# Branch A of a hybrid attention trunk: one softmax over the keys of three groups, with layouts swapped by small matmuls on TensorE

## The chip, the cores and the metric
One core of one Trainium2 chip runs the whole program. The metric is the device time of one execution in microseconds (us), as a median over runs. PE is the engine of matmuls (TensorE), DVE is VectorE, ACT is ScalarE, POOL is GpSimd, and SP issues the DMAs.

## What is computed
Two layers over 512 tokens of width 1024, batch 1, all in fp32. Each layer normalizes and modulates x, projects it once (w_in), and runs two branches on the result. Branch A, which the change touches, is attention with 8 heads of 64 in each of three groups with different windows and dilations; the groups' results are mixed per query by their softmax denominators. From the reference:

```python
A_PATTERNS = ((128, 1), (512, 4), (2048, 16))
...
    s = jnp.where(valid[None, None, :, None], s + bias, NEG_INF)
    m = jnp.max(s, axis=-1, keepdims=True)
    p = jnp.exp(s - m)
    l = jnp.sum(p, axis=-1, keepdims=True)
    o = jnp.einsum('bpnhqk,bpnkhd->bpnqhd', (p / l).astype(v.dtype), vw)
    lse = (m + jnp.log(l))[..., 0]
...
    wts = jax.nn.softmax(jnp.stack(lses), axis=0)
    o = jnp.sum(jnp.stack(outs).astype(jnp.float32) * wts[..., None], axis=0)
```

Weighting the groups by a softmax of lse = m + log l is the same as one softmax over all keys of the three groups: the sum of exp(s - M) v over all groups, divided by the sum of exp(s - M). Branch B is latent attention with 16 heads. Gates, the two output projections, a merge and w_o follow, and x is added.

## The kernel before
Activations lie transposed, with channels on partitions and tokens along the free axis. Matmul operands are split into a high and a low part in fp32r, so that a product takes three matmuls (hi x hi, hi x lo, lo x hi), and nearly every PSUM result is evacuated twice: ACT (or DVE) copies the high part, DVE subtracts it for the low part. PSUM has tags with few banks: pj 2 (projections), s 3 (scores), t 2 (transposes, statistics), o 1 (results).

A layer runs branch A in four passes, j = 0 to 3, each with two heads (e = 0, 1) of all three groups. a_qk(j) projects queries and keys, six projections of 24 matmuls each, from bank pj; line 663 writes the low part of a key of groups 1 and 2, line 671 of a query of those groups. a_v projects values, zgate the gate z. a_attn(j) then calls a_scores, a_factors and, for each head, a_pv and o_evac, and multiplies by z.

Group 0 is in the order of tokens: queries are split into four blocks of 128 consecutive tokens. Groups 1 and 2 are in the order of phases: block p holds the tokens 4i + p. Within a block of group 0 the queries are ordered so that partition 32p + a holds phase p. So a statistic of query block qb, phase p lies on partitions 32p.. in column qb for group 0, and on partitions 32qb.. in column p for groups 1 and 2. swap_blocks (line 812) goes from one layout to the other by sixteen copies of 32 partitions, twelve on DVE and four on POOL.

In a_scores each group takes its own maximum (line 779 adds the bias and takes the maximum of group 0 in one DVE instruction, line 797 that of groups 1 and 2), and ACT computes the exponentials with that maximum and sums them along the way (lines 783 and 803). a_factors joins the two maxima and sums of groups 1 and 2 (lines 822 to 827), swaps them, joins them with group 0 (lines 831 to 846), swaps the common factor back and forms three factors per query. a_pv scales every block of the probabilities with its factor (scaled, line 859; on DVE, POOL and ACT by the table SE), transposes the blocks on PE (line 866), splits them into pth (line 211) and ptl (line 869), and multiplies with the values in bank o.

The instructions of each engine stand in the order that a scheduler gives them when the program is built, by its own estimate of durations; so work of the next a_qk stands between the steps of a_attn. An engine takes them strictly in that order. Line 166 is the helper of every matmul, line 211 and 213 the copies of high parts, lines 203, 205 and 206 split loaded weights (206 is the subtraction, mostly on POOL).

## Time and profile before

| what | us |
| --- | --- |
| median of 3 runs (1478.69 to 1481.86) | 1481.09 |
| the profiled execution, its own time | 1478.29 |
| its span, first to last instruction | 1476.5 |
| PE busy in it | 1369.5 |
| DVE busy | 1004.1 |
| ACT busy | 624.0 |
| POOL busy | 601.3 |

The span is 1.8 us under the profiled execution's own time, which is 2.8 us under the median. Branch A of layer 0 lies at about 120 to 450 us of the span, that of layer 1 at about 800 to 1150 us. The passes of a_factors are at 173, 228, 366, 417, 883, 941, 1067 and 1117 us. Busy times of engines overlap; a matmul's record is longer than the distance to the next one, since matmuls are pipelined.

### The profile page before, as it was taken

Reading aid. Unit: us, or ns where it says so; the run is one execution under the profiler, and the core shown is the slowest. Engines: PE = TensorE matmul, PEld = TensorE weight load, DVE = VectorE, ACT = ScalarE, POOL = GpSimd, SP = SyncE. Lnnn points to the kernel's source line nnn. Section 1 sums busy time; section 2 is a strip of 40 time slices with the busy share of each in tenths; the row PEclk is TensorE's granted clock in tenths of the full one; section 3 lists DMA queues with packets and bytes.
Section 4 is the critical chain, followed back from the end, with each engine's and each line's share of the span. In section 5 each row is a group of like instructions: output and inputs, shape, how many; then the busy total and the mean of one; then the engine's idle time right before and its main releaser. Section 6 shows DMA issues by size and latency. Waiting matters only on the chain.

```text
span 1476.5 us, 21392 instructions
## 1 busy us (share of the span) xinstructions
PE 1369.5 (93%) x7327; PEld 1161.5 (79%) x7327; DVE 1004.1 (68%) x2477; ACT 624.0 (42%) x1493; POOL 601.3 (41%) x493
## 2 busy tenths in 40 slices
PE   5998898999998998999989999899999899899997
PEld 4786686897777787888888987789777778788877
DVE  8788759345776888764699347734576688885563
ACT  3423552325245767621034254323534566762101
POOL 4423435234463323245544344533446433335530
PEclk7999999999999999999999999999999999999999
DMA  9776414232244333355654322233323442345551
GB/s 323 230 232 189 140 44 117 81 85 79 59 116 122 99 94 95 117 178 171 199 159 135 102 86 71 67 88 86 79 72 110 116 115 79 94 120 188 171 150 58
DMA packets 236677, 181.48 MB, mean 123 GB/s; under 512 B 16410, under 2 KB 204224, under 8 KB 236568
## 3 DMA queue, kind: packets, MB, share of 16 engines
q1 hardware_dynamic: 236568, 180.11, 41.2%
q8 instruction: 58, 0.95, 0.3%
q14 instruction: 51, 0.42, 0.1%
HBM read 150.60 MB, written 23.17 MB: 118 GB/s over the span
## 4 chain that ended last, share of the span: by engine, by line
PE 62%; DVE 21%; ACT 4%; issue 4%; DMA 4%; POOL 3%; SPq 1%; DVEq 0%; POOLq 0%; ACTq 0%
PE pj L166 41%; PE s L166 14%; PE o L166 4%; PE t L866 3%; ACT p L803 2%; DVE mn L812 2%; POOL wl L206 2%; DVE ptl L869 1%; DVE p L1098 1%; DVE lat L286 1%; DVE zs L286 1%; DVE wh L205 1%; DMA stage<-in_w_o 1%; DMA stage<-in_w_in 1%; DVE fp L812 1%
## 5 line engine op out<-in xcount | busy, mean ns | idle before, releaser
L206 POOL TENSOR_TENSOR wl<-stage,wh 128x1024 fp32r<-128x1024 f32 (+1 forms) x134 | 316.7, 2364 | 353.5 <-ACT wh L203 188.8
L166 PE MATMUL pj<-hTh,wh 128*128 128x512 f32 (+1 forms) x864 | 346.5, 401 | 44.7 <-DVE kb L663 19.9
L166 PE MATMUL pj<-hTl,wh 128*128 128x512 f32 (+1 forms) x864 | 339.4, 394 | 0.0
L166 PE MATMUL pj<-hTh,wl 128*128 128x512 f32 (+1 forms) x848 | 336.9, 397 | 0.0
L166 PEld LDWEIGHTS pj<-hTh,wh 128*128 128x128 f32 x864 | 166.2, 192 | 85.1 <-issue 31.8
L166 PEld LDWEIGHTS pj<-hTl,wh 128*128 128x128 f32 x864 | 165.9, 192 | 32.6 <-issue 0.3
L166 PEld LDWEIGHTS pj<-hTh,wl 128*128 128x128 f32 x848 | 163.2, 192 | 29.6 <-issue 0.2
L203 ACT ACTIVATE wh<-stage 128x1024 fp32r<-128x1024 f32 (+1 forms) x84 | 85.1, 1014 | 155.4 <-PE s L166 62.7
L869 DVE TENSOR_TENSOR ptl<-t,pth 128x512 fp32r<-128x512 f32 (+2 forms) x160 | 95.9, 615 | 44.0 <-ACT pth L211 43.4
L211 ACT ACTIVATE pth<-t 128x512 fp32r<-128x512 f32 (+2 forms) x160 | 80.8, 537 | 63.2 <-PE t L866 61.9
L166 PE MATMUL s<-kb,qh 128*128 128x256 f32 (+3 forms) x384 | 86.3, 317 | 7.6 <-DVE mm L1098 3.6
L166 PE MATMUL o<-pth,v 128*64 128x128 f32 (+3 forms) x496 | 88.7, 256 | 3.3 <-DVE kh L920 1.9
L166 PE MATMUL o<-ptl,v 128*64 128x128 f32 (+2 forms) x320 | 77.2, 275 | 6.8 <-DVE ptl L869 6.3
L866 PE MATMUL t<-eye_r,p 128*128 128x128 f32 x560 | 80.1, 275 | 2.7 <-DVE ptl L869 1.0
L166 PEld LDWEIGHTS s<-kb,qh 128*128 128x128 f32 x384 | 65.0, 189 | 18.7 <-DVE mm L1098 6.2
L1098 DVE CUSTOM_DVE_ANT_0 p<-s,cs 128x512 f32<-128x512 f32 (+3 forms) x128 | 58.5, 484 | 25.9 <-PE s L166 25.4
L205 DVE CAST wh<-stage 128x1024 fp32r<-128x1024 f32 (+1 forms) x77 | 57.2, 743 | 25.4 <-PE s L166 8.4
L166 PEld LDWEIGHTS o<-pth,v 128*64 128x64 f32 (+1 forms) x496 | 63.7, 150 | 9.7 <-DVE kh L920 3.2
L866 PEld LDWEIGHTS t<-eye_r,p 128*128 128x128 f32 x560 | 63.2, 140 | 9.9 <-DVE p L859 2.4
L166 PE MATMUL pj<-wh,hTh 128*128 128x256 f32 (+1 forms) x192 | 63.3, 331 | 3.5 <-DVE p L972 1.8
L166 PE MATMUL pj<-wl,hTh 128*128 128x256 f32 (+1 forms) x192 | 62.4, 327 | 1.0 <-DVE wl L206 0.8
L166 PEld LDWEIGHTS o<-ptl,v 128*128 128x128 f32 (+1 forms) x320 | 50.8, 159 | 14.8 <-DVE ptl L869 10.4
(711 smaller groups left out, 3088.1 us busy)
## 6 DMA issues: line engine op xcount, KB each, us to landing
stage<-in_w_in SPq DMA_DIRECT2D x118, 512.0 KB
lat<-in_w_ada SPq DMA_DIRECT2D x64, 256.0 KB
v<-in_w_ada SPq DMA_DIRECT2D x32, 256.0 KB
stage<-in_w_in SPq DMA_DIRECT2D x32, 256.0 KB
gd<-gt SPq DMA_DIRECT2D x32, 256.0 KB
stage<-in_w_out_b SPq DMA_DIRECT2D x16, 512.0 KB
stage<-in_w_o SPq DMA_DIRECT2D x16, 512.0 KB
p<-yd SPq DMA_DIRECT2D x24, 256.0 KB
```

The lines of the kernel that those rows point to most:

```text
L166: T.matmul(o, l, r, start=start, stop=stop, skip_group_check=True)
L203: A.activation(dst_h, src, AF.Copy)
L205: hi.tensor_copy(dst_h, src)
L206: (lo or G).tensor_tensor(dst_l, src, f32(dst_h), ALU.subtract)
L211: A.activation(dst, src, AF.Copy)
L286: V.scalar_tensor_tensor(acc, st, cact[:, k:k + 1], side if k == ne + np_ else acc, ALU.mult, ALU.add)
L803: A.activation(pt[e][:, sl], pt[e][:, sl], AF.Exp, bias=m12[:, g - 1, e, p:p + 1], scale=SA, accum_out=l12[:, g - 1, e, p:p + 1])
L812: (A.copy if c == "A" else (G if c == "G" else V).tensor_copy)(dst[32 * p:32 * p + 32, :, qb], src[32 * qb:32 * qb + 32, :, p])
L866: T.transpose(tp[:, 128 * b:128 * b + 128], s, eye)
L869: V.tensor_tensor(lo[:, :n], tp[:, :n], f32(h[:, :n]), ALU.subtract)
L1098: V.tensor_tensor_reduce(pt, o, mask[:, 512 - n:512], 1.0, -3e38, ALU.add, ALU.max, m[:, qb:qb + 1])
```

## The change
In a_scores, groups 1 and 2 now come first, then group 0. The maximum over groups 1 and 2 (mx) goes into the layout of group 0 by swapped(): DVE multiplies it into ex with a mask (quad) that leaves each value in one of four columns by its quarter of the partitions, and one fp32 matmul with the 0/1 matrix blk (1 where two partitions agree modulo 32) sums over the quarters, so that every quarter holds all values; four instructions of 32 partitions then pick what they need straight from PSUM. M is the maximum over all three groups, its negated and scaled form nM goes back by a second swapped() (nM12), and all exponentials use it: those of group 0 with nM, those of groups 1 and 2 with nM12. No block of probabilities is scaled. a_factors and swap_blocks are gone. a_inverse adds the sums of the groups (with a third swapped()), takes the reciprocal, transposes it (8 x 128), and spreads it with four fp32 matmuls (rowsel is 0/1, 8 rows) over the 128 partitions of the result's layout, in PSUM; the gate z is multiplied by that before it multiplies the result. Three constant tables come with it, in cs (blk, quad) and in rowsel, and the reserve in SBUF for DMA descriptors is set to 1024 bytes a partition.

```diff
+        def swapped(v):
+
+            ex = small([128, 2, 4, 4], "ex")
+            st = list(v.ap[0])
+            a = bass.AP(tensor=v.tensor, offset=v.offset, ap=[st, [4, 2], [1, 4], [0, 4]])
+            m = bass.AP(tensor=quad.tensor, offset=quad.offset, ap=[list(quad.ap[0]), [0, 2], [0, 4], [1, 4]])
+            V.tensor_tensor(ex, a, m, ALU.mult)
+            ps_ = bank("t")
+            mm(ps_[:, :32], blk, ex.rearrange("p e c b -> p (e c b)"), True, True)
+            r = ps_[:, :32].rearrange("p (e c b) -> p e c b", e=2, c=4)
+            return [(slice(32 * c, 32 * c + 32), r[32 * c:32 * c + 32, :, c, :]) for c in range(4)]
...
-                V.tensor_scalar(m0[:, e, :], x0, -SA, None, ALU.mult)
-                for qb, pc, c0, n in G0_BLOCKS:
-                    A.activation(pp[pc][:, c0:c0 + n], pp[pc][:, c0:c0 + n], AF.Exp, bias=m0[:, e, qb:qb + 1],
-                                 scale=SA, accum_out=l0[:, e, qb:qb + 1])
-                pps[e] += pp
...
+            mx = small([128, 2, 4], "mx")
+            V.tensor_tensor(mx, x12[:, 0], x12[:, 1], ALU.max)
+            other = swapped(mx)
...
+            M = small([128, 2, 4], "M")
+            for r, v in other:
+                V.tensor_tensor(M[r], x0[r], v, ALU.max)
+            nM = small([128, 2, 4], "nM")
+            V.tensor_scalar(nM, M, -SA, None, ALU.mult)
+            nM12 = small([128, 2, 4], "nM12")
+            for r, v in swapped(nM):
+                V.tensor_copy(nM12[r], v)
+            l0, l12 = small([128, 2, 4], "l0"), small([128, 2, 2, 4], "l12")
+            for e in range(2):
+                for g in (1, 2):
+                    pt = pps[e][1 + g]
                     for p in range(4):
                         sl = slice(128 * p, 128 * p + 128)
-                        A.activation(pt[e][:, sl], pt[e][:, sl], AF.Exp, bias=m12[:, g - 1, e, p:p + 1],
+                        A.activation(pt[:, sl], pt[:, sl], AF.Exp, bias=nM12[:, e, p:p + 1],
                                      scale=SA, accum_out=l12[:, g - 1, e, p:p + 1])
...
+                for qb, pc, c0, n in G0_BLOCKS:
+                    pt = pps[e][pc][:, c0:c0 + n]
+                    A.activation(pt, pt, AF.Exp, bias=nM[:, e, qb:qb + 1], scale=SA, accum_out=l0[:, e, qb:qb + 1])
+            return pps, l0, l12
+
+        def a_inverse(l0, l12):
+
+            V.tensor_tensor(l12[:, 0], l12[:, 0], l12[:, 1], ALU.add)
+            for r, v in swapped(l12[:, 0]):
+                V.tensor_tensor(l0[r], l0[r], v, ALU.add)
+            V.reciprocal(l0, l0)
+            tp = bank("t")
+            T.transpose(tp[:8, :128], l0.rearrange("p e t -> p (e t)"), eye)
+            rw = small([8, 128], "rw")
+            V.tensor_copy(rw, tp[:8, :128])
+            bc = bank("t")
+            for t in range(4):
+                mm(bc[:, 128 * t:128 * t + 128], rowsel[:, 128 * t:128 * t + 128], rw, t == 0, t == 3)
+            return bc
...
-            for pc in range(2):
-                scaled(pp[pc], [(c0, n, f0[:, qb:qb + 1]) for qb, pc_, c0, n in G0_BLOCKS if pc_ == pc], SE[pc])
...
-                scaled(pp[1 + g], [(128 * p, 128, f12[:, g - 1, p:p + 1]) for p in range(4)], SE[1 + g])
...
-            pps = a_scores(j, qk, stat)
-            f0, f12 = a_factors(stat)
+            pps, l0, l12 = a_scores(j, qk)
+            zn = z.rearrange("d (t a q) -> d t q a", t=4, q=4)
             for e in range(2):
-                o = a_pv(e, pps[e], f0[:, e], f12[:, :, e], vt, 2 * (j % 2) + e)
+                o = a_pv(e, pps[e], vt, 2 * (j % 2) + e)
+                if e == 0:
+                    V.tensor_tensor(zn, zn, a_inverse(l0, l12).rearrange("d (t q a) -> d t q a", t=4, q=4), ALU.mult)
                 o_evac(y, e, o, True)
...
-    nc = bacc.Bacc("TRN2", target_bir_lowering=False, num_devices=1)
+    nc = bacc.Bacc("TRN2", target_bir_lowering=False, num_devices=1, dynamic_dma_scratch_size=1024)
```

The scheduler moves more than the diff shows. In what follows, numbers behind a name tell buffers apart, and line numbers of the changed kernel are its own.

On DVE, in the first pass of layer 0, the twelve copies of the first swap stand ahead of the low part of a key (kb, line 663):

```order
L812 COPY mn_1362<-ml_1353 32x4 x12
L663 TENSOR_TENSOR kb_447<-pj_1740,kb_444 64x4x128
L213 CAST kb_444<-pj_1740 64x4x128
L831 TENSOR_TENSOR M_1379<-m_265_1232,mn_1362 128x8
L663 TENSOR_TENSOR kb_447<-pj_1740,kb_444 64x4x128
L833 TENSOR_TENSOR en_1381<-M_1379,m_265_1232 128x8
L834 TENSOR_TENSOR en_1381<-M_1379,mn_1362 128x8
```

In the changed kernel, at the same key (line 670 there), after the maximum:

```order
L694 TENSOR_TENSOR k_353_1643<-pj_1616,kh_1641 64x512
L820 TENSOR_TENSOR M_1327<-x_280_1294,t_1292 32x8 x4
L822 TENSOR_SCALAR nM_1332<-M_1327 128x8
L768 TENSOR_TENSOR ex_1335<-nM_1332,cs 128x32
L694 TENSOR_TENSOR k_353_1643<-pj_1616,kl_1642 64x512
L825 COPY nM_291_1334<-t_1337 32x8 x4
L670 TENSOR_TENSOR kb_448<-pj_1691,kb_445 64x4x128
L217 CAST kb_445<-pj_1691 64x4x128
L670 TENSOR_TENSOR kb_448<-pj_1691,kb_445 64x4x128
```

Ahead of the key now stand the four maxima of 32 partitions (M), the negation, the product with the mask (ex), the low part of a key of the next pass's group 0, and the four copies from PSUM (nM).

On ACT, at the same place before, the exponentials of groups 1 and 2 (line 803) stand ahead of the high part of that key (kb) and of a query (qh); those of group 0 were done before them:

```order
L803 ACTIVATE p_1286,l_268_1235<-p_1286,m_267_1234 128x128 x4
L803 ACTIVATE p_1287,l_268_1235<-p_1287,m_267_1234 128x128 x4
L277 ACTIVATE lat_1851<-lat_1851,cact 128x512
L203 ACTIVATE wh_1806<-stage_1804 128x1024
L803 ACTIVATE p_1320,l_268_1235<-p_1320,m_267_1234 128x128 x4
L803 ACTIVATE p_1321,l_268_1235<-p_1321,m_267_1234 128x128 x4
L824 ACTIVATE ed_1355<-ed_1355 128x16
L211 ACTIVATE kb_444<-pj_1740 64x4x128
L203 ACTIVATE wh_2242<-stage_2240 128x1024
L211 ACTIVATE qh_1800<-pj_1775 128x512
```

In the changed kernel, from the second head's exponentials of group 0 (line 836) on; those of groups 1 and 2 are line 832:

```order
L836 ACTIVATE p_1313,l_294_1343<-p_1313,nM_1332 128x256 x2
L836 ACTIVATE p_1314,l_294_1343<-p_1314,nM_1332 128x256
L836 ACTIVATE p_1314,l_294_1343<-p_1314,nM_1332 128x128
L215 ACTIVATE kb_445<-pj_1691 64x4x128
L207 ACTIVATE wh_2142<-stage_2140 128x1024
L832 ACTIVATE p_1240,l_295_1344<-p_1240,nM_291_1334 128x128 x4
L832 ACTIVATE p_1264,l_295_1344<-p_1264,nM_291_1334 128x128 x4
L832 ACTIVATE p_1241,l_295_1344<-p_1241,nM_291_1334 128x128 x4
L832 ACTIVATE p_1265,l_295_1344<-p_1265,nM_291_1334 128x128 x4
L215 ACTIVATE pth_1375<-t_1370 128x512
L215 ACTIVATE pth_1387<-t_1383 128x384
L215 ACTIVATE qh_1751<-pj_1726 128x512
```

The key's copy moved in between the two blocks of exponentials, and the query's copy (qh) behind both, and behind two copies of transposed blocks (pth).

On PE, the first transposes of the pass's probabilities stood 73 projection matmuls behind its last score:

```order
L166 MATMUL pj_2246<-hTl_219,wh_2242 128x512
L166 MATMUL pj_2246<-hTh_220,wh_2242 128x512
L866 MATMUL t_1419<-eye_r,p_1245 128x128
L866 MATMUL t_1419<-eye_r,p_1244 128x128 x3
L866 MATMUL t_1432<-eye_r,p_1244 128x128
L866 MATMUL t_1432<-eye_r,p_1245 128x128 x2
L166 MATMUL pj_2246<-hTh_220,wl_2243 128x512
```

In the changed kernel they stand seven matmuls behind the second swapped() (t<-ex), which itself stands 24 projection matmuls behind the pass's last score, one of group 0:

```order
L170 MATMUL t_1337<-ex_1335,cs 128x32
L170 MATMUL pj_1726<-hTh_210,wh_1722 128x512
L170 MATMUL pj_1726<-hTh_210,wl_1723 128x512
L170 MATMUL pj_1726<-hTl_211,wh_1722 128x512
L170 MATMUL pj_1726<-hTh_212,wh_1722 128x512
L170 MATMUL pj_1726<-hTh_212,wl_1723 128x512
L170 MATMUL pj_1726<-hTl_213,wh_1722 128x512
L170 MATMUL pj_1726<-hTh_214,wh_1722 128x512
L868 MATMUL t_1370<-eye_r,p_1298 128x128
L868 MATMUL t_1370<-eye_r,p_1297 128x128 x3
L170 MATMUL pj_1726<-hTh_214,wl_1723 128x512
```

The transposes moved forward, from 73 to 31 projection matmuls behind the last score, and the matmul with ex is new. Matmuls and projections of the latent-attention stages stand as before.

## Rows read from the trace of the kernel before

**Rows 1.** The page's engines (busy us, share, instructions), and its chain by engine.
```profile
PE 1369.5 (93%) x7327; PEld 1161.5 (79%) x7327; DVE 1004.1 (68%) x2477; ACT 624.0 (42%) x1493; POOL 601.3 (41%) x493
...
PE 62%; DVE 21%; ACT 4%; issue 4%; DMA 4%; POOL 3%; SPq 1%; DVEq 0%; POOLq 0%; ACTq 0%
```

**Rows 2.** Windows: us, then each engine's busy us (instructions), PEclk, DMA share, GB/s.
```profile
170.00:300.00 130.00, 116.09 (x623) 95.85 (x622) 84.83 (x228) 48.98 (x125) 51.46 (x56) 0.95 0.32 90
...
450.00:740.00 290.00, 276.73 (x1434) 231.33 (x1434) 210.89 (x469) 138.12 (x315) 115.08 (x85) 1.00 0.46 135
```

**Rows 3.** PE's waits: us in total, times, longest us.
```profile
PE pj L166 <- DVE kb L663: 21.5, 10, 4.5
...
PE o L166 <- DVE ptl L869: 6.3, 13, 1.0
```

**Rows 4.** PE's timeline at eight gaps: start us, us, instruction [idle before <-releaser].
```profile
181.06 0.77 PE L166 MATMUL pj<-hTh,wh 128*128 128x512 f32 x1 [4.46 <-DVE kb L663]
...
237.03 0.57 PE L166 MATMUL pj<-hTh,wh 128*128 128x512 f32 x1 [3.87 <-DVE kb L663]
...
253.49 0.47 PE L166 MATMUL pj<-hTh,wh 128*128 128x512 f32 x1 [1.92 <-DVE kb L663]
...
373.44 0.47 PE L166 MATMUL pj<-hTh,wh 128*128 128x512 f32 x1 [1.89 <-DVE kb L663]
...
889.72 0.47 PE L166 MATMUL pj<-hTh,wh 128*128 128x512 f32 x1 [1.40 <-DVE kb L663]
...
898.29 0.50 PE L166 MATMUL pj<-hTh,wh 128*128 128x512 f32 x1 [1.26 <-DVE ql L671]
...
956.68 0.47 PE L166 MATMUL pj<-hTh,wh 128*128 128x512 f32 x1 [4.08 <-DVE kb L663]
...
1074.11 0.47 PE L166 MATMUL pj<-hTh,wh 128*128 128x512 f32 x1 [1.90 <-DVE kb L663]
```

**Rows 5.** Timeline of DVE and POOL at the first swap of layer 0.
```profile
173.20 4.38 DVE L812 COPY mn<-ml 32x4 f32<-32x4 f32 x12
...
174.45 2.38 POOL L206 TENSOR_TENSOR wl<-stage,wh 128x1024 fp32r<-128x1024 f32 x1 [0.37 <-POOL mn L812]
...
177.61 0.68 DVE L663 TENSOR_TENSOR kb<-pj,kb 64x512 fp32r<-64x512 f32 x1
```

**Rows 6.** Tile mn: engine op xcount: duration ns min/median/max, first and last start us, forms.
```profile
L812 DVE COPY mn<-ml x96: 160/164/2403, 173.2 to 1118.9; 32x4 f32<-32x4 f32 x96
```

**Rows 7.** Windows behind PE's gaps and one at full clock; columns as in rows 2.
```profile
181.06:186.06 5.00, 5.00 (x12) 3.94 (x13) 4.65 (x25) 0.21 (x1) 1.93 (x6) 0.50 0.39 105
...
186.20:191.20 5.00, 5.00 (x23) 4.13 (x22) 3.55 (x13) 2.82 (x6) 4.05 (x7) 1.00 0.00 0
...
237.26:240.67 3.41, 3.41 (x9) 2.64 (x9) 3.38 (x12) 1.10 (x3) 0.40 (x1) 0.50 0.72 193
...
957.47:960.88 3.41, 3.41 (x10) 2.63 (x9) 0.84 (x2) 0.00 (x0) 3.33 (x3) 0.50 0.38 100
```

**Rows 8.** Groups of DVE and ACT by form: xcount | busy us, mean ns.
```profile
L812 DVE COPY mn<-ml 32x4 f32<-32x4 f32 x96 | 27.5, 287 | 1.4
...
L812 DVE COPY fp<-fn 32x2 f32<-32x2 f32 x96 | 19.3, 201 | 1.5
...
L803 ACT ACTIVATE p<-p,m 128x128 f32<-128x128 f32 x128 | 49.6, 389 | 23.3 <-DVE m L799 23.2
...
L783 ACT ACTIVATE p<-p,m 128x256 f32<-128x256 f32 x48 | 23.9, 499 | 22.4 <-DVE m L781 22.1
...
L211 ACT ACTIVATE pth<-t 128x512 fp32r<-128x512 f32 x112 | 63.4, 592 | 62.3 <-PE t L866 61.4
```

**Rows 9.** PE's timeline: fp32 matmuls at full clock, early in the program.
```profile
47.60 0.95 PE L166 MATMUL t<-one_r,zs 128*128 128x1 f32 x8
...
64.98 1.68 PE L166 MATMUL t<-yy,rb 32*24 32x512 f32 x4
```

**Rows 10.** The page's costliest groups: GpSimd's subtraction.
```profile
L206 POOL TENSOR_TENSOR wl<-stage,wh 128x1024 fp32r<-128x1024 f32 (+1 forms) x134 | 316.7, 2364 | 353.5 <-ACT wh L203 188.8
```

96 lines of the change are left out of this document (29 added, 67 removed).

## The prediction

> **What bounds the kernel now.** I first read the engine summary and the chain that ended last: PE is busy for 1369.5 of 1476.5 us and holds 62% of the chain, against 21% for DVE [rows 1]. So time is what PE does plus what PE waits. The busy times by stretch then separate the stages: in the first branch-A stage of layer 0 (170 to 300 us) PE stands idle for 130.00 - 116.09 = 13.9 us, over a tenth, while in the latent-attention stage (450 to 740 us) it stands idle for 13.3 us in 290 [rows 2]. The list of PE's waits says for whom: first comes DVE's line 663, the low part of a projected key, which must be read out of a pj bank before PE may start the next projection; 21.5 us in 10 waits [rows 3]. PE's timeline has eight gaps beside the eight passes through a_factors: 4.46, 3.87, 1.92 and 1.89 us in layer 0, and 1.40, 1.26, 4.08 and 1.90 us in layer 1, 20.8 us together [rows 4]. Seven are line 663, one is line 671, the same work for a query.
>
> Why line 663 is late stands in the timeline of DVE at 173 us [rows 5]. It is queued behind the twelve 32-partition copies of swap_blocks, 4.38 us of DVE, and starts at 177.61, the moment they end. A copy of this tile takes 164 ns at the median but up to 2403 [rows 6], and twelve at the median would be 2.0 us: the other 2.4 us of the 4.38 are those for which GpSimd worked on a 128x1024 subtraction, from 174.45 for 2.38 us [rows 5]. The four larger gaps come with the copies of that first swap, or with the second swap and the row scalings behind it.
>
> A gap costs more than itself. [...] Beside the a_factors passes there are 5.00 us at 0.50 from 181.06, and four stretches of 3.41 us (the first and the last are [rows 7], the others start at 254.33 and 373.80): 18.6 us in which PE did 12/23 of the work, so 18.6 x 0.48 = 8.9 us lost.
>
> **What the change takes away.** Both swaps go, and with them twelve plus twelve DVE copies per attention, 27.5 + 19.3 us over eight attentions [rows 8], some twenty small DVE operations, and every row scaling of the probabilities, which ran on DVE, ACT and POOL. The order of the changed kernel has line 663 behind four short PSUM copies where it had the twelve. I therefore cancel all eight gaps, -20.8 us, and their slow clock, -8.9 us. The rest of DVE's saved time I cost at nothing: PE had no gap there, because projections covered it.
>
> **What it adds on PE.** Nothing that PE did is removed, and PE is the bound, so each added matmul counts in full. Per attention: three products of the 128x128 matrix blk with 32 columns; one transpose; four spreading matmuls with 8 rows and 128 columns. These are fp32, not fp32r. The trace holds two records for an fp32 matmul: four program matmuls with one column are eight records, 0.95 us [rows 9], so 0.24 us each; I take that for a product, 3 x 0.24 = 0.72. The four records of a 32-row fp32 matmul took 1.68 us for 2 x (512 + 384) = 1792 columns [rows 9], 0.94 ns a column; spreading passes 4 x 2 x 128 = 1024 columns, 0.96 us. The transpose is one record, 0.95/8 = 0.12 us. Together 1.8 us, and with eight attentions +14.5 us. From below this is 0, if all of it falls into waits that remain; from above it is twice as much, 29 us, were every added matmul to run at the lower clock; I stay at the row's value because the products stand among projections that keep PE busy. [...]
>
> **What it adds as waits.** The exponentials now share one maximum. All 24 of an attention start only after scores, maximum, product, maximum, and, for groups 1 and 2, a second product. Before, the eight of group 0 could run ahead of the rest. ACT's part is 16 x 0.389 + 6 x 0.499 + 2 x 0.389 = 10.0 us in two blocks, 3.8 and 6.2 [rows 8]. What must not wait behind them is ACT's copy of the next projection (pth and qh in the order of ACT). In the first attention I count from the negated maximum: 3.8 (eight exponentials), 0.6 for kb, 1.1 for one weight cast, 6.2, then two copies of transposed blocks and qh, 0.6 each, and 0.7 on DVE: free after 14.2 us (an ACT copy of a transposed block is 592 ns [rows 8], a weight cast of 1024 columns taken as nearly twice that, DVE's part 0.68 us [rows 5]). PE meanwhile has from the last score 24 projection matmuls, the product, then 48 more, 7 transposes and a few scores before it needs the bank: 72 x 0.217 (5.00/23 [rows 7]) = 15.6, plus some 1.6 for the others at 0.12 each, 17.2 us from the last score. The maximum comes about 2 us after the last score (one reduction, five short operations at about 0.2 us [rows 8], and other work between). Slack: about 1 us. So no systematic wait, but little room. I charge one wait per attention of the kind that the latent-attention stage shows for the same handover, PE for DVE's ptl: 6.3 us in 13 waits, 0.48 us [rows 3]; eight of them, with a little for the bank of tag t that a product holds until the maximum is read, +5 us. Bounds: 0 (cover holds) and 22 us (first rival).
>
> DVE's new operations are 21 short ones and one 512-column product per attention, about 21 x 0.2 + 0.7 = 4.9 us (a short copy of fp took 201 ns on the mean, the 0.7 is line 663's for 512 columns), less than the 5.9 us of the copies alone ((27.5 + 19.3)/8 [rows 8]), and no PE projection waits for the 512-column product. One more DMA, rowsel, and 132 more columns of cs are loaded once, long before use. The smaller reserve for DMA descriptors is at nothing: the loads are issued by SP, and no row shows a use of it. In the latent-attention stages PE's order is that of before, so there I expect no change.
>
> **Sum.** -20.8 - 8.9 + 14.5 + 5 = -10.2. The profiled execution took 1478.29 us (1476.5 us of span and 1.8 around it), 2.8 us under the median of three runs, 1481.09. From the median: **1471 us**.
>
> **Rivals.**
> 1. *ACT's block becomes the wait* (slower). If the maximum arrives late against PE, so that the eight exponentials of group 0 no longer hide, the bank comes 3.8 us later, PE waits 3.8 - 1.0 = 2.8 us in each attention, 22 us in place of the 5: 1488 us. It decides from the point where the maximum is more than that 1 us later than I count. For it: the slack is small, and PE will arrive earlier once its own gaps are gone. Against: in the order of the changed kernel 48 projection matmuls stand between the second product and the first use of the blocks that need it, and ACT is busy for only 624 us [rows 1].
> 2. *The small operations are caught by GpSimd* (no change). A DVE copy stood up to 2.4 us where GpSimd subtracted [rows 5, 6]. The change keeps six such SBUF operations per attention in front of the products (maximum, three products with quad, a sum, a negation), 48 in all. GpSimd's subtraction fills 316.7 of 1476.5 us, 21%, 2364 ns each [rows 10], so an operation meets one with chance 0.21 and stands half of it: 48 x 0.21 x 1.18 = 12 us; if PE waits for all that on top of the forecast: 1483 us. Against it: the median copy of the swap took 164 ns [rows 6], so most were not held, and projections cover the product. [...]
> 3. *The added matmuls fall into remaining waits*, and no new wait comes: -5 - 7 against the sum, 1459 us.
>
> **How the numbers follow.** The forecast (1463 to 1478) has 0.60, rival 3 0.15, rival 1 0.13, rival 2 0.12, of which I put 0.02 with slower. A difference under about 3 us (0.2%) can't be told from none. So faster 0.75, same 0.10, slower 0.15. The range for 8 in 10 goes from a little under rival 3 to a little over rival 1: 1457 to 1490 us.
>
> **What would show it.** Right: line 663 gone from the head of PE's waits, branch-A stretches 29 us shorter in gaps and slow clock but PE's busy time up by 10 to 20 us, DVE's busy time down by tens of us, no granted clock of 0.50 after the first 150 us of layer 0 except at the seams of layers. Wrong by rival 1: PE waiting on ACT's copies or on line 671 behind exponentials, 2 us or more, once per attention. Wrong by rival 2: short operations of over 1 us on DVE ahead of each product, with PE waiting at t<-ex. Wrong on the price: the fp32 records longer than 0.12 us apart.

## The result, and the profile after

The changed kernel takes **1494.47 us** (median of 4 runs, 1489.08 to 1496.09) where the kernel before takes 1481.47 us beside it: ratio 1.0075, 95% interval 1.0048 to 1.0101. It is slower by 13 us; the forecast was 10 us faster. Measured once more beside other kernels the ratio was 1.0076 (1.0062 to 1.0091).

The page's engines and its chain by engine, of the kernel after:

```profile
PE 1389.2 (93%) x7447; PEld 1178.2 (79%) x7447; DVE 956.5 (64%) x2197; ACT 613.0 (41%) x1445; POOL 540.7 (36%) x365
...
PE 70%; DVE 16%; DMA 4%; issue 4%; ACT 3%; SPq 2%; POOL 2%; DVEq 0%; ACTq 0%; POOLq 0%
```

Against [rows 1], DVE is busy for 48 us less and its share of the chain has fallen from 21% to 16%, as the change intended. But PE is busy for 19.7 us more, and its idle time, span less busy time, has fallen only from 107.0 to 1493.6 - 1389.2 = 104.4 us. PE's waits in the kernel after (us in total, times, longest us; helper lines stand four to seven lines further down than before, so that line 663 is now 670, 671 is 678, and 687 is 694):

```profile
PE o L170 <- DVE ptl L871: 8.6, 15, 1.0
...
PE pj L170 <- DVE k L694: 6.7, 2, 4.8
...
PE pj L170 <- DVE ql L678: 5.4, 4, 4.1
PE pj L170 <- DVE ex L768: 4.4, 1, 4.4
...
PE pj L170 <- DVE kb L670: 1.7, 2, 1.3
```

The head of [rows 3], line 663 with 21.5 us, has shrunk to 1.7 us in two waits (line 670). In its place stand other reads of projections (a group-0 key in line 694, a query in line 678) and a product's input (line 768), each with one gap of more than 4 us. The new idle time doesn't come once per attention: branch A has seven gaps of more than 1 us, 20.9 us together, and they belong to five of the eight attentions. These are five of the seven (the others are 1.47 and 1.98 us, at 423 and 1137 us):

```profile
226.67 0.79 PE L170 MATMUL pj<-hTh,wh 128*128 128x512 f32 x1 [4.80 <-DVE k L694]
...
247.81 0.47 PE L170 MATMUL pj<-hTh,wh 128*128 128x512 f32 x1 [4.09 <-DVE ql L678]
...
878.28 0.77 PE L170 MATMUL pj<-hTh,wh 128*128 128x512 f32 x1 [4.38 <-DVE ex L768]
...
940.88 0.42 PE L170 MATMUL o<-lat,one_r 128*2 128x512 f32 x1 [2.24 <-DVE yy L919]
...
943.64 0.80 PE L170 MATMUL pj<-hTh,wh 128*128 128x512 f32 x1 [1.92 <-DVE k L694]
```

The slow clock is there again. Two windows (columns as in [rows 2]), one that begins inside the gap before 878.28 and one that begins between the two gaps around 941, show the granted clock at 0.50 for 6.83 us each; PE worked at that level for 4.80 and 4.91 us of them, against 5.00 and 3.41 us in [rows 7].

```profile
876.25:883.08 6.83, 4.80 (x11) 3.80 (x12) 2.68 (x4) 3.83 (x16) 1.87 (x2) 0.50 0.28 77
941.11:947.94 6.83, 4.91 (x12) 3.44 (x11) 5.19 (x11) 3.25 (x12) 3.94 (x3) 0.50 0.39 98
```

Over the whole span the time at this lower level went from 65.1 to 81.4 us. A second profile of the changed kernel has 75.8 us, with 104.6 us of idle time, so the figure at the lower level varies by some us between executions of one kernel.

How such a gap comes about is read from three engines at 873 us, in the first attention of layer 1. First PE, from the pass's last score (s) on: two projection matmuls, and behind the gap the one at 878.28 that is shown above. Then DVE, then GpSimd:

```profile
872.91 0.32 PE L170 MATMUL s<-k,ql 64*128 64x128 f32 x1
873.16 0.50 PE L170 MATMUL pj<-hTh,wl 128*128 128x512 f32 x1
873.50 0.40 PE L170 MATMUL pj<-hTl,wh 128*128 128x512 f32 x1
```

```profile
873.27 0.29 DVE L815 CUSTOM_DVE_ANT_0 p<-s,bias 128x128 f32<-128x128 f32 x1 [3.06 <-PE s L170]
873.49 0.08 DVE L815 DVE_READ_ACCUMULATOR2_ANT x<- 128x1 f32 x1
873.49 0.68 DVE L694 TENSOR_TENSOR k<-pj,kh 64x512 fp32r<-64x512 f32 x1
874.09 0.67 DVE L820 TENSOR_TENSOR M<-x,t 32x8 f32<-32x8 f32 x4
874.78 0.69 DVE L217 CAST qh<-pj 128x512 fp32r<-128x512 f32 x1
875.50 2.04 DVE L822 TENSOR_SCALAR nM<-M 128x8 f32<-128x8 f32 x1
877.46 0.68 DVE L678 TENSOR_TENSOR ql<-pj,qh 128x512 fp32r<-128x512 f32 x1
878.06 0.18 DVE L768 TENSOR_TENSOR ex<-nM,cs 128x32 f32<-128x32 f32 x1
```

```profile
875.17 2.34 POOL L210 TENSOR_TENSOR wl<-stage,wh 128x1024 fp32r<-128x1024 f32 x1 [4.79 <-issue]
```

DVE first stands idle for 3.06 us, because the last reduction is next in its order and PE has not yet made that score; the read behind it (line 694), whose high part ACT had written by 869.48, starts only at 873.49. Then everything behind it comes at once: a projection's read, the common maximum M, another read, the negation, one more read of a projection (line 678), and the product's input, which the trace names as the releaser. The negation of 128x8 takes 2.04 us where its shortest takes 0.17; it ends 0.03 us after GpSimd's subtraction, which runs from 875.17 to 877.51. The projection for which PE stands needs a bank that these reads free; it starts 0.14 us after the query's read (line 678) has ended and 0.04 us after the product's input. The other gaps have other blockers in the same queue. Ahead of 226.67 DVE waits only 0.50 us for a score, and then five reads of banks, the maximum M and the negation, held for 0.6 us, stand in a row. Ahead of 247.81 the query's read stands behind the inverse's sum and mask and behind a sum over other loaded weights (line 290) that had to wait for its DMA:

```profile
245.52 0.75 DVE L290 SCALAR_TENSOR_TENSOR lat<-lat,cact,lat 128x512 f32<-128x512 f32 x1 [1.09 <-DMA lat<-in_w_ada]
```

### The profile page after: what moved, and what is told of

The parts are those of the page before. It is cut to its first block, busy times and chain, and to the rows that moved or that the text cites. A ratio compares the mean times of both kernels' runs of the same rounds, so it can differ in the third digit from the quotient of the medians.

```text
span 1493.6 us, 21132 instructions
## 1 busy us (share of the span) xinstructions
PE 1389.2 (93%) x7447; PEld 1178.2 (79%) x7447; DVE 956.5 (64%) x2197; ACT 613.0 (41%) x1445; POOL 540.7 (36%) x365
## 4 chain that ended last, share of the span: by engine, by line
PE 70%; DVE 16%; DMA 4%; issue 4%; ACT 3%; SPq 2%; POOL 2%; DVEq 0%; ACTq 0%; POOLq 0%
PE pj L170 48%; PE s L170 12%; PE o L170 4%; PE t L868 3%; PE t L170 1%; DMA stage<-in_w_o 1%; DVE p L1097 1%; DVE ptl L871 1%; POOL wl L210 1%; DMA stage<-in_w_in 1%; DVE kb L1039 1%; DMA lat<-in_w_ada 1%; DVE lat L290 1%; DVE wh L209 1%; DVE wl L210 1%
## 5 line engine op out<-in xcount | busy, mean ns | idle before, releaser
L868 PE MATMUL t<-eye_r,p 128*128 128x128 f32 x560 | 84.9, 276 | 6.5 <-DVE nM L825 3.4
L170 PE MATMUL o<-ptl,v 128*64 128x128 f32 (+2 forms) x320 | 78.7, 278 | 9.1 <-DVE ptl L871 8.6
L290 DVE SCALAR_TENSOR_TENSOR lat<-lat,cact,lat 128x512 f32<-128x512 f32 x56 | 56.6, 1011 | 18.1 <-ACT lat L281 6.1
```

What stands on the lines that cost most here:

```text
L170: T.matmul(o, l, r, start=start, stop=stop, skip_group_check=True)
L290: V.scalar_tensor_tensor(acc, st, cact[:, k:k + 1], side if k == ne + np_ else acc, ALU.mult, ALU.add)
L868: T.transpose(tp[:, 128 * b:128 * b + 128], s, eye)
```

## The experiments

Times in text are medians; steps between kernels that ran on different chips are taken from the ratios to the kernel before, times 1481.09 us. Removed and added lines are shown, and "..." marks lines left out. Each edit lets the scheduler place the work anew, also where nothing was edited: of the edited kernels below only the one with the smaller reserve has exactly the order of the kernel that it is compared with.

### What the removed part was worth, and the swap by itself

The first kernel leaves out a_factors and all row scalings of the kernel before, and with them the common maximum and the division by the sums:

```
-                scaled(pp[pc], [(c0, n, f0[:, qb:qb + 1]) for qb, pc_, c0, n in G0_BLOCKS if pc_ == pc], SE[pc])
...
-                scaled(pp[1 + g], [(128 * p, 128, f12[:, g - 1, p:p + 1]) for p in range(4)], SE[1 + g])
...
-            f0, f12 = a_factors(stat)
```

> The kernel before without a_factors and without the row scalings: own maxima, nothing rescaled, no division (left out: the common maximum and the division). It shows what the prediction's step 'cancel all eight gaps and their slow clock' is worth by itself: 20.8 + 8.9 us by that step, so 1451 us, PE idle 86 us. If a new pile-up on DVE takes the place of the old one whatever stands there: 1465 us or more. Against the changed kernel without the inverse (1457 us), which has two products and 0.3 us more of PE work per attention (3 us) and one common maximum: equal but for these 3 us if the common maximum makes no wait, 10 us or more below if it does.

Measured: 1439.97 us, ratio 0.9726 (0.9698 to 0.9753). Its page's engines, and what is left of the waits for line 663:

```profile
PE 1359.1 (95%) x7327; PEld 1158.1 (81%) x7327; DVE 909.6 (63%) x2061; ACT 613.3 (43%) x1445; POOL 544.5 (38%) x365
...
PE pj L166 <- DVE kb L663: 1.6, 2, 1.3
```

With 1437.8 us of span PE's idle time is 78.7 us, 28.3 less than before, and the time at the lower clock is 50.7 us, 14.4 less; line 663 keeps 1.6 of its 21.5 us. So the step "cancel all eight gaps" is right, if a little short: removing gives 40.6 us, not 29.7, as long as nothing comes in its place.

The second keeps maxima, factors and scalings of the kernel before, and replaces only the twelve copies of each swap by one product and four copies from PSUM:

```
-            for qb in range(4):
-                for p in range(4):
...
-                        dst[32 * p:32 * p + 32, :, qb], src[32 * qb:32 * qb + 32, :, p])
...
+            V.tensor_tensor(ex, a, m, ALU.mult)
+            ps_ = bank("t")
+            mm(ps_[:, :16 * n], blk, ex.rearrange("p e c b -> p (e c b)"), True, True)
...
+            for c in range(4):
+                V.tensor_copy(dst[32 * c:32 * c + 32], r[32 * c:32 * c + 32, :, c, :])
```

> The kernel before, with its own maxima, factors and scalings, where only the sixteen copies of each swap are replaced by one product with the mask, one fp32 matmul and four copies from PSUM. The prediction's step (the copies on DVE make the gaps): some 15 of the 20.8 us of gaps and 6 us of slow clock go, two matmuls per pass add 3 us, 1463 us. Theory A (a gap goes to whatever stands ahead of the evacuation next): 1475 to 1482 us. Theory C: 1484 us.

Measured: **1456.47 us, ratio 0.9840 (0.9816 to 0.9865)**. It is faster than both kernels. So the swap by a matmul does not make the changed kernel slow by itself; the rest of the change does. In this kernel, too, the key reads of branch A (line 666 here, 663 before) no longer lead PE's waits; those of the latent stage stand above them:

```profile
PE pj L168 <- DVE kb L1049: 5.0, 8, 1.6
...
PE pj L168 <- DVE kb L666: 4.0, 4, 1.3
```

Ten waits of up to 4.5 us have become four of up to 1.3.

In it GpSimd's subtractions for the branch-A weights were then moved to DVE (`qk="AVAV", v="AVAV"`).

> The kernel before with its swap copies replaced by products (1456 us), and in it GpSimd's subtractions for the weights of queries, keys and values moved to DVE. The many short operations of its factors read SBUF; nothing would hold them any more. If holding still costs there: 1450 us or less. If DVE's added 90 us cost more than the holding: 1460 us or more.

Measured: 1464.91 us, 0.9896 (0.9868 to 0.9924), so 8 us worse than without. There DVE's added work, or the order that comes with it, costs more than whatever GpSimd's holding does. And the kernel before with only the smaller descriptor reserve (`dynamic_dma_scratch_size=1024`):

> The kernel before with only the smaller reserve for DMA descriptors that the change also sets. The prediction put this at nothing: 1481 us, ratio 1.000 within 0.2%, PE idle 107 us as before. If the reserve had a cost or a gain of its own, the latent-attention stages would move too: a ratio outside 0.998 to 1.002.

Measured: 1481.45 us, 1.0005 (0.9989 to 1.0022): nothing, as the prediction had it. This one has the order of the kernel before, instruction by instruction, on PE and DVE.

### What each added part costs

The changed kernel without a_inverse and the gate's product, so that it has the common maximum and no division:

```
-                if e == 0:
-                    V.tensor_tensor(zn, zn, a_inverse(l0, l12).rearrange("d (t q a) -> d t q a", t=4, q=4), ALU.mult)
```

> The changed kernel without a_inverse and the product of the gate with it: the result of branch A is not divided by the sums. Left out per pass: one product, one small transpose, four spreading matmuls, some eight short DVE operations and one of 512 columns. Theory C: PE loses some 1.4 us per pass, 11 us in all, 1483 us, and PE's gaps stay. Theory A: the gaps behind the maximum stay (about 40 us of gaps in branch A of both layers), and the time lies at 1481 to 1486 us, the price alone. If waits of a_inverse itself on DVE counted as well, it would come below 1478 us.

Measured: 1456.88 us, 0.9843 (0.9822 to 0.9864). This is a surprise on both sides: the inverse costs over 30 us, and the common maximum alone costs 17 us against the kernel without factors, though it adds only two small products per attention and the other order of the groups. The 4.38 us gap is still in the list of PE's waits of this kernel, so it belongs to the maximum:

```profile
PE pj L170 <- DVE ex L768: 4.4, 1, 4.4
```

Then the inverse in steps. Its PE work alone, on constants (idle is a tile of zeros), in the kernel without it:

```
+                if e == 0:
+                    mm(bank("t")[:, :32], blk, idle[:, :32], True, True)
+                    T.transpose(bank("t")[:8, :128], idle[:, :8], eye)
+                    bc = bank("t")
+                    for t in range(4):
+                        mm(bc[:, 128 * t:128 * t + 128], rowsel[:, 128 * t:128 * t + 128], idle[:8], t == 0, t == 3)
```

> The changed kernel without the inverse of the sums (1457 us), but with the PE work of it: at the same place, on constants, a product of 128x32, an 8-column transpose and the four spreading matmuls, which wait for nothing and which nothing reads. Left out is the division by the sums. Their duration by the trace is 0.16 + 0.1 + 1.2 us, eight times, 12 us. If PE's added time is the price and the rest of the inverse's 36 us are waits of its chain on DVE: 1467 to 1470 us. If the added matmuls themselves (with the bank of transposes that they take, and the clock behind them) are the whole: 1485 us or more. If they hide in PE's waits: 1457 to 1461 us.

Measured: 1471.58 us, 0.9948 (0.9925 to 0.9970), 15.6 us above the kernel without it. PE is busy for 1378.7 us against 1367.3: 11.4 us, about what the records of the kernel after say for the spreading and a third of the products (groups by form, xcount | busy us, mean ns):

```profile
L170 PE MATMUL t<-rw,rowsel 8*128 8x128 f32 x64 | 9.2, 283 | 0.0
...
L170 PE MATMUL t<-ex,cs 128*128 128x32 f32 x48 | 7.8, 243 | 0.0
```

The chain without the spreading and the gate's product:

```
             V.tensor_copy(rw, tp[:8, :128])
-            bc = bank("t")
-            for t in range(4):
-                mm(bc[:, 128 * t:128 * t + 128], rowsel[:, 128 * t:128 * t + 128], rw, t == 0, t == 3)
-            return bc
...
+                    a_inverse(l0, l12)
```

> The changed kernel with the inverse's chain up to the copy of the transposed reciprocals, but without the four spreading matmuls and without the gate's product (left out: the division by the sums). Between the kernel without any inverse (1457 us) and the one that spreads it but does not apply it (1480 us). If the spreading's 1.2 us of PE per attention is the price: 1470 us here, and the chain costs 13 us by waits. If the chain on DVE is what makes PE wait: 1477 us or more. If neither does and the order of the work decides: 1460 us or less.

Measured: 1472.78 us, 0.9956 (0.9938 to 0.9974): a chain with some 3 us of PE work (a third of the 7.8 us above, and a transpose) costs 16.8 us; in the profiles 5.3 us of that are idle time and 10.1 us more are spent at the lower clock. With the spreading, but not applied to the gate:

```
-                    V.tensor_tensor(zn, zn, a_inverse(l0, l12).rearrange("d (t q a) -> d t q a", t=4, q=4), ALU.mult)
+                    keep = a_inverse(l0, l12)
+                    V.tensor_copy(small([128, 1], "kp"), keep[:, :1])
```

> The changed kernel with the inverse of the sums computed and spread over the bank, but not multiplied onto the gate (only one column of it is read, so that the bank is kept as long as needed): left out is the division of the result by the sums. Leaving out the whole inverse gave 36 us, of which about 10 are its matmuls on PE. If the 1.1 us product on DVE per attention, with what stands behind it, makes the other 26: about 1466 us. If the chain ahead of it does (a sum, a mask, four additions, a reciprocal, a copy, each between two PE operations): about 1485 us.

Measured: 1479.67 us, 0.9998 (0.9984 to 1.0011), between the two expectations, nearer to the second. The ladder, with idle time and time at the lower clock from the profiles:

| kernel | ratio to before | us by ratio | PE busy | PE idle | at clock 0.50 |
|---|---|---|---|---|---|
| before | 1 | 1481.1 | 1369.5 | 107.0 | 65.1 |
| no factors, no scaling | 0.9726 | 1440.5 | 1359.1 | 78.7 | 50.7 |
| + common maximum | 0.9843 | 1457.8 | 1367.3 | 88.5 | 65.1 |
| + chain of the inverse | 0.9956 | 1474.6 | 1376.8 | 93.8 | 75.2 |
| + spreading | 0.9998 | 1480.8 | 1383.0 | 96.0 | 69.6 |
| + gate's product = after | 1.0076 | 1492.3 | 1389.2 | 104.4 | 81.4 |

The last step, 11.5 us, is one DVE operation per attention, which lasts 1.1 us. DVE also stands still ahead of it:

```profile
L928 DVE TENSOR_TENSOR zs<-zs,t 128x512 f32<-128x512 f32 x8 | 8.8, 1103 | 13.7 <-PE t L170 13.7
```

Which of the two is it, the operation or the stop? In the kernel that doesn't apply the inverse, the one-column copy stops DVE for the same 13.7 us, and the 11.5 us are not paid. So it is not the stop by itself. The next kernel takes the product off DVE:

```
-                    V.tensor_tensor(zn, zn, a_inverse(l0, l12).rearrange("d (t q a) -> d t q a", t=4, q=4), ALU.mult)
...
+                    A.activation(iv, a_inverse(l0, l12), AF.Copy)
+                    G.tensor_tensor(zn, zn, iv.rearrange("d (t q a) -> d t q a", t=4, q=4), ALU.mult)
```

> The changed kernel with the product of the gate and the spread inverse taken off DVE: ACT copies the bank to SBUF (some 0.6 us), GpSimd multiplies (some 1.3 us). If the 13 us that the applied product costs are its 1.1 us on DVE, in front of what PE waits for: 1480 us. If they are the time for which the bank of transposes is held until the product has read it: about the same or, with ACT behind its exponentials, above 1492 us.

Measured: 1480.76 us, 0.9997 (0.9982 to 1.0012): the 11.7 us come back, though ACT now stands in DVE's place and GpSimd takes 1.5 us for each product (source line of the copy: duration, and what ended ACT's idle time before it):

```profile
L929 ACT ACTIVATE iv<-t x8: 597/598/599, 203.7 to 1151.2; 128x512 f32<-128x512 f32 x8
its engine sat idle before it (us, times) until:
  PE t L170: 21.2, 6
```

That DVE's 1.1 us is the price agrees with both runs, but they don't show it. PE itself waits for the product for only 1.4 us in all; the rest of the 11.5 us is idle time and slow clock elsewhere, as at the two gaps around 941 us, and the order of DVE's work differs in each of these kernels: of the changed kernel's 1869 DVE operations some 240 stand elsewhere in this one, of its 7447 matmul records only 43. A later place for the same work helps, too, but less; here a_inverse and the product stand behind both heads:

```
-                if e == 0:
-                    V.tensor_tensor(zn, zn, a_inverse(l0, l12).rearrange("d (t q a) -> d t q a", t=4, q=4), ALU.mult)
                 o_evac(y, e, o, True)
+            V.tensor_tensor(zn, zn, a_inverse(l0, l12).rearrange("d (t q a) -> d t q a", t=4, q=4), ALU.mult)
```

> The changed kernel with the inverse of the sums, and the product of the gate with it, moved behind the attention's two heads (it stood between them). The work is the same. Leaving it out altogether gave 34 us, of which some 11 are its own matmuls (0.16 us for the product, 0.1 for the transpose, 1.2 for the spreading, eight times). If the other 23 us are waits that come from its place between the heads, where PE's next transposes need the bank and DVE's next copies stand behind the 1.1 us gate product: about 1471 us. If they come from its DVE operations wherever these stand: about 1490 us. If at the end it delays the last matmul of each pair of heads and the next projection's gate: above 1494 us.

Measured: 1482.87 us, 1.0023 (1.0009 to 1.0037), 8 us less than the changed kernel by their ratios. Of the 23 us that the first expectation looked for in the place, a third is there; this is the same work in another order, so order alone is worth 8 us here. Cheaper spreading, by writing each reciprocal into 64 columns and transposing four blocks:

```
-            T.transpose(tp[:8, :128], l0.rearrange("p e t -> p (e t)"), eye)
...
-            V.tensor_copy(rw, tp[:8, :128])
...
+                V.reciprocal(lv[:, :, e, :], l0[:, e, :].unsqueeze(2).to_broadcast([128, 4, 64]))
...
-                mm(bc[:, 128 * t:128 * t + 128], rowsel[:, 128 * t:128 * t + 128], rw, t == 0, t == 3)
+                T.transpose(bc[:, 128 * t:128 * t + 128], lw[:, 128 * t:128 * t + 128], eye)
```

> The changed kernel, with the spreading done otherwise: the reciprocal is written 64 times over into 512 columns, and four transposes with the unit matrix carry it into the result's layout; no small transpose, no copy, no matmuls with 8 rows. Price: eight records at 0.126 us, the change of shape behind them 0.2 us and a transpose go, four transposes at 0.11 us come, 0.85 us less per pass, 7 us in all: 1487 us by theories A, B and C alike. If the matmuls with 8 rows cost more than their spacing (the clock falls behind them), 1483 us or less; if they lay in waits, 1494 us.

Measured: 1478.65 us, 0.9999 (0.9986 to 1.0013): 11 us less than the changed kernel, where 7 were expected. It does so although its reciprocals of 256 columns take DVE 1.73 us each, sixteen times, 27.7 us of work in front of the gate's product where 3.8 us stood before; so work added to DVE has no fixed price.

### The operations that GpSimd holds

In the kernel after, most kinds of short operations that read SBUF alone have long ones among them, and those that read PSUM have none (source lines; duration ns min/median/max):

```profile
L802 DVE TENSOR_TENSOR mx<-x x8: 167/1248/2353, 150.5 to 1107.1; 128x8 f32<-128x8 f32 x8
```

```profile
L822 DVE TENSOR_SCALAR nM<-M x8: 172/594/2035, 166.9 to 1130.5; 128x8 f32<-128x8 f32 x8
```

```profile
L820 DVE TENSOR_TENSOR M<-x,t x32: 139/155/169, 166.2 to 1130.3; 32x8 f32<-32x8 f32 x32
```

Against its shortest, the maximum loses 7.7 us in eight, the masks 7.7 in 24, the negation 5.5 in eight, the sum 3.7 in eight: 24.6 us of DVE. Nineteen of these operations take over 0.3 us, and each of the nineteen ends 0.02 to 0.05 us after an operation of GpSimd that ran beside it. Of the 96 operations with an input from PSUM 48 ran beside one of its weight subtractions, and none took more than 173 ns. But holding doesn't tell the kernels apart: in the kernel of 1456 us, which has only its swaps replaced, the short operations of a_factors and its swaps lose some 26 us, 9.0 of them in one line:

```profile
L840 DVE TENSOR_TENSOR M<-m,mn x8: 157/1840/2341, 179.3 to 1092.3; 128x8 f32<-128x8 f32 x8
```

The first experiment takes the negation away, by forming it in the four operations that read PSUM (quad_n is the mask times -SA):

```
-            other = swapped(mx)
+            other = swapped(mx, quad_n)
...
-                V.tensor_tensor(M[r], x0[r], v, ALU.max)
...
-            V.tensor_scalar(nM, M, -SA, None, ALU.mult)
+                V.scalar_tensor_tensor(nM[r], x0[r], -SA, v, ALU.mult, ALU.min)
```

> The changed kernel, but the negated maximum comes straight out of the four short operations that read PSUM (a second mask holds -1/8 in place of 1), so the separate negation on DVE, which GpSimd's subtraction held for up to 2.0 us, is gone. Theory A (PE waits because projections' evacuations stand on DVE behind the chain of the maximum, whatever is in it): PE's gaps stay about as many, 1490 to 1494 us. Theory B (short DVE operations held by GpSimd make the gaps): the gaps of 4.4 and 1.9 us in layer 1 shrink by 2 and 1.5 us and with them goes slow clock, 1485 to 1488 us. Theory C (the time is the price of the added matmuls alone): no change, 1494 us.

Measured: 1476.35 us, 0.9977 (0.9964 to 0.9991): some 15 us less, nearly three times what was held. In the gap near 874 us the mask of the product was now caught in the negation's stead (2.06 us), and 3.72 us of the gap stayed. So this gain can't be the hold at that place.

The second leaves two of the six: group 2's reductions start from group 1's maximum, the second product's input is written from PSUM, and both halves of the sums go through one product.

```
+                                                   1.0, -3e38 if g == 1 else x12[:, 0, e, p:p + 1], ALU.add, ALU.max,
...
+                V.scalar_tensor_tensor(exn[r, :, :, c], x0[r], -SA, v, ALU.mult, ALU.min)
...
-            V.tensor_tensor(l12[:, 0], l12[:, 0], l12[:, 1], ALU.add)
+            for r, v in swapped(l12, 4):
```

> The changed kernel with two instead of six short operations per attention that read only SBUF on DVE: the maximum of groups 1 and 2 is folded into the reductions of group 2 (which start from the maximum of group 1), the negated maximum and the masked input of the second product are both written straight from PSUM (four operations more), and both halves of the sums go through one product. Held in the changed kernel: 24.6 us in all on DVE (maximum 7.7, masks 7.7, negation 5.5, sum 3.7); some 8 to 11 would be left. Theory A (PE's new gaps are made by operations that GpSimd's subtraction holds): the 4.4 us gap near 874 us goes, PE idle falls by some 15 us or more, 1470 us or less. Theory B (the gaps are made by the length of the chain on DVE, which stands behind casts and reads of projections in the order, and the hold is only a part): the gap near 874 us keeps 2 us or more, 1474 to 1484 us. Theory C (the shorter chain is placed still nearer to the scores in PE's order, so that PE waits as long): 1490 us.

Measured: 1482.06 us, 1.0009 (0.9998 to 1.0021). Holding fell from 24.6 to 5.6 us, the time by 10 us. PE's timeline at the same place:

```profile
875.39 0.41 PE L171 MATMUL t<-exn,cs 128*128 128x32 f32 x2 [0.71 <-DVE exn L824]
878.23 0.47 PE L171 MATMUL pj<-hTh,wh 128*128 128x512 f32 x1 [2.43 <-DVE ql L682]
```

Nothing is held here, and PE still stands for 0.71 + 2.43 = 3.1 us. Theory B, that the hold is a part and the length of DVE's chain the rest, fits best. The third moves GpSimd's weight subtractions of branch A to DVE (`qk="AVAV", v="AVAV"`):

> The changed kernel with GpSimd's subtractions for the weights of queries, keys and values moved to DVE: about 61 fewer on GpSimd, at 1.57 us each on DVE by the 26 that run there already, so DVE is busy for 90 us more (some 1050 us). Nothing is then held beside most of the products. Theory A (the holding is what makes PE wait): the short operations stay under 0.3 us, PE's gaps at the products go, 1470 us or less, if DVE's added work hides. Theory B (DVE's queue is what makes PE wait, whatever holds it): each product now stands behind a 1.57 us subtraction instead of a 2.4 us hold, and so do the reads of the projections: 1495 to 1520 us, PE idle over 105 us.

Measured: 1477.38 us, 0.9979 (0.9968 to 0.9990), DVE 979.0 us busy. Neither theory had it, and it was no clean test: DVE's busy time rose by 22 us where 90 were expected, and GpSimd's other work still held short operations for 17 us. The gap near 874 us is gone, and another one is there, in which only the negation is held, for 0.6 us (DVE's timeline):

```profile
921.13 0.29 DVE L815 CUSTOM_DVE_ANT_0 p<-s,bias 128x128 f32<-128x128 f32 x1 [5.12 <-PE s L170]
921.34 0.08 DVE L815 DVE_READ_ACCUMULATOR2_ANT x<- 128x1 f32 x1
921.34 0.68 DVE L694 TENSOR_TENSOR k<-pj,kh 64x512 fp32r<-64x512 f32 x1
921.95 0.66 DVE L820 TENSOR_TENSOR M<-x,t 32x8 f32<-32x8 f32 x4
922.64 1.05 DVE L217 COPY yy<-o 64x512 f32<-64x512 f32 x1
923.73 0.68 DVE L670 TENSOR_TENSOR kb<-pj,kb 64x512 fp32r<-64x512 f32 x1
924.42 0.69 DVE L217 CAST kb<-pj 64x512 fp32r<-64x512 f32 x1
925.15 0.77 DVE L822 TENSOR_SCALAR nM<-M 128x8 f32<-128x8 f32 x1
925.95 0.69 DVE L694 TENSOR_TENSOR k<-pj,kl 64x512 fp32r<-64x512 f32 x1
```

PE waits 4.81 us here, for the last row. DVE had stood idle for 5.12 us in front of a reduction whose score was not there, with five reads of banks behind it.

### Gains that don't add

The kernels of this part put edits together that stand above; the changed kernel ran once more beside the first.

| edits on the changed kernel | us | ratio |
|---|---|---|
| none (once more) | 1492.50 | 1.0076 (1.0062 to 1.0091) |
| no negation, spreading by transposes | 1481.06 | 1.0005 (0.9991 to 1.0019) |
| two of six SBUF operations, inverse late, transposes | 1490.04 | 1.0057 (1.0038 to 1.0076) |
| no negation, gate's product on GpSimd | 1473.92 | 0.9952 (0.9935 to 0.9969) |

> The changed kernel itself once more, beside the others on one chip, so that their differences to it need no detour. All theories: 1494 us, ratio 1.0075 to the kernel before, within 0.3%.

> The changed kernel with two edits that were run one by one: the negated maximum is formed straight from the four PSUM operations (no separate negation on DVE), and the inverse sums are spread by four 128x128 transposes instead of a transpose, a copy and four 8-row matmuls. Theory A (each edit took away its own waits of PE in front of a product or of the spreading, so they add): 1494 - 18 - 16, about 1460 us, PE idle about 80 us. Theory B (only the first edit takes away a wait, the second only its 1.0 us of fp32 matmuls per attention): about 1469 us. Theory C (each edit gained because the whole order of the instructions came out differently, not by its own waits, so that two edits are not better than one): 1474 to 1480 us, PE idle about 90 us.

> All edits that each helped the changed kernel, together: the two-operation chain of the run before last, the inverse behind the attention's two heads, and its spreading by four transposes. If the gains come from their own waits: under 1465 us, PE idle 80 us or less. If the design with one maximum stays bound by the product that PE waits for in each attention: 1470 to 1480 us, not better than the kernel before with only its swaps replaced (1456 us).

> The same on the changed kernel without the separate negation (1476 us). If the two are waits of their own: 1464 us. If what is won once is not won again, as in the two combinations before: 1474 to 1482 us. In either case not below the kernel before with its swaps replaced by products (1456 us).

Only the last pair is better than its parts (1476 and 1481 us), by 2 to 4 us, and its interval touches that of the better part. The first is no better than either alone, and the third, with the fewest held operations of all, is almost back at the changed kernel. Each edit makes the scheduler order the whole of branch A anew, and gaps appear at other places: in the third, two of 4.2 us in front of the transposes of the reciprocals. So of the 8 to 15 us that every single edit on the changed kernel won, how much is the edit's own wait and how much a luckier order stays open; no run here fixes the order of one kernel and changes the other. The steps of the ladder carry the same doubt, a few microseconds each; their sum doesn't. None of these kernels comes near the 1456 us of the kernel with only its swaps replaced.

## Why the prediction was wrong

**What is taken away: right, and short.** Predicted -20.8 for the gaps and -8.9 for their clock; without factors, swaps and scalings, and with nothing in their place, the kernel gains 40.6 us, 28.3 of it PE's idle time, and 14.4 us fewer are spent at the lower clock (6.9 us lost, at the prediction's 0.48, which is 1 - 12/23 by the matmuls that start in 5.00 us at 0.50 and at 1.00 in [rows 7]).

**What is added on PE: right.** Predicted 14.5 us, 1.8 per attention. The records give 9.2 us for the spreading and 7.8 for the 24 products, whose ends overlap what follows, and the inverse's PE work alone adds 11.4 us of busy time (15.6 us of time). From the kernel without factors to the changed one, the span grows by 1493.6 - 1437.8 = 55.8 us; 104.4 - 78.7 = 25.7 of it is idle time, and (81.4 - 50.7) x 0.48 = 14.7 the lower clock, with the prediction's own 12/23; the 15.4 that remain are the work. The terms of the second profile of the changed kernel differ by up to 3 us.

**What is added as waits: this step failed.** It read "I charge one wait per attention of the kind that the latent-attention stage shows for the same handover [...] +5 us". Instead of 5 us there are 25.7 us of idle time and 14.7 us of lower clock behind it, some 40 us. Three things went wrong in it. It counted the cover in the first attention only (24 projections behind the last score) and took it for all eight. In that attention the count held, for no gap of more than 1 us follows; at 873 us two projections follow the last score, and then PE has to wait for a bank. It followed ACT's queue, which ends none of the seven gaps; PE waits for DVE, where the reads of the projections stand in one order with the reductions, the maximum and the inverse. Of that order it took only four short copies to stand ahead of the key, though the order in "The change" has eleven instructions there. And it gave the new gaps no slow clock, though it had given one to the old ones. "No PE projection waits for the 512-column product" belongs here: the product, priced at 0.7 us, lasts 1.1, PE's direct waits for it are 1.4 us, and the kernel with it takes 11.5 us more. How the 40 us divide between the chain's length, the holding and the order that the scheduler happened to give stays open.

**The rivals.** The time came out nearest the first rival's figure, 1488 us, but not by its mechanism: ACT's exponentials make no gap of 2 us once per attention. The second rival's mechanism is there, larger than worked out (24.6 us of DVE instead of 12), and it had a chance of 0.12; but a gap of 3.1 us outlives it where nothing is held, and a kernel with as much holding takes 1456 us. In the trace the maximum, the masks and the sum, which have two inputs in SBUF, took up to 2.35 us, the negation, which has one, up to 2.04 us, and the 96 operations of 32 partitions that read PSUM stay under 0.18 us; what sets them apart no row shows. The third rival fell: the inverse's matmuls alone cost 15.6 us and hide in no wait.

**The list of signs.** Line 663 left the head of PE's waits, PE's busy time rose by 19.7 us and DVE's fell by 47.6, all as listed; the clock of 0.50 did not go away but grew, and short operations of over 1 us stand on DVE. In the trace of the kernel after the eight records of one spreading start 0.126 us apart on the mean, and the two of a product 0.03 to 0.13 us, mostly 0.03. So the 0.12 us read from one-column records is not the distance within a product; a product was priced somewhat high and the spreading somewhat low, and the price was not the error.

## What to carry to other kernels

When a change replaces one stall by a chain that hops between in-order engines, price every place where the chain's links stand in front of work that the bound engine waits for, in each iteration and not only in the first, and add to each new gap the slow clock that the old gaps had (here 3.41 to 6.83 us at 0.50). Leave the new part out altogether, then add its links one by one: here that showed in five kernels that removing was worth 41 us and adding cost 52. And try the smallest piece of a change alone: the swap by a matmul, without the redesign around it, was 1.6% faster than the kernel before. Where a scheduler orders the program anew after every edit, take gains of single edits that don't add as a sign of that order, here 8 us for one piece of work moved.

## What the runs showed of the hardware

A 128x8 operation on DVE that lasts 0.17 us took up to 2.35 us beside a subtraction of 2.3 to 2.5 us on GpSimd. This held for the negation, with one input in SBUF (2.04 us), and for the maximum, with two. In the changed kernel it never happened to its operations of 32x8 with an input from PSUM: the longest of 96 took 173 ns, and 48 of them ran beside such a subtraction.

In the changed kernel three stretches in which the granted clock was 0.50 lasted 6.83 us around gaps of branch A; two began inside the gaps of 4.80 and 4.38 us, the third between those of 2.24 and 1.92 us. Of the five such stretches at the gaps of [rows 4], before the change, one lasted 6.83 us and four 3.41.

DVE stands still for 13.7 us in front of the spread inverse both in the kernel of 1480 us and in that of 1492 us, so this stop alone does not make the difference. Nor does added work on DVE have a fixed price: 8.8 us of it came with 11.5 us more, and 27.7 us of it, in place of other work on PE and DVE, with 11 us less.
